# One transformer layer on one core: parameters packed by the host, the order of the first loads, and the stage's stored activations loaded by ScalarE's queue

## The chip, the core and the metric

The kernel runs on one core of a Trainium2 chip. The metric is the device time of one execution in microseconds (us). A core has five engines that work through their own instruction lists in order: TensorE (PE, matmuls), VectorE (DVE), ScalarE (ACT), GpSimd (POOL) and SyncE (SP, which here only issues DMAs). An engine whose instruction waits holds back everything behind it in its list. A DMA is issued by an instruction in some engine's list and then carried out by the core's 16 DMA engines.

## What is computed

One layer over 1024 tokens of width 1024: an adaptive RMSNorm, one projection that feeds eight attention heads and eight RWKV-7 heads, their output projection, and a PEER block, a feed-forward layer with 16,384 single-neuron experts of which each token uses 128.

```python
mod = silu(c) @ ada_w + ada_b                  # shift1, scale1, gate1, shift2, scale2, gate2
h   = rms_norm(x, norm1_g) * (1 + scale1) + shift1
z   = h @ w_in                                 # attention and RWKV-7 heads work on z
x   = x + gate1 * (concat(att, rw) @ w_out)
h2  = rms_norm(x, norm2_g) * (1 + scale2) + shift2
...
def block(args):                               # PEER, a block of 128 tokens; ic are the chosen experts
    u = take(expert_u, ic)
    act = gelu(einsum('cd,ced->ce', xc, u), approximate=False)
    vv = take(expert_v, ic)
    return einsum('ce,ced->cd', gc * act, vv)
```

## The kernel before

**The front** (0 to some 65 us). Small parameters are loaded one by one, each laid over partitions by the DMA itself: `scol` (L117) by SP, `bcol`, `g1col`, `mup`, `mun` and four pieces of `gqk` (L119 to L129) by ACT's queue, `w0`, `a0`, `kkc`, `kac`, `rkc` through `colp` (L319 to L322) by POOL's. DVE builds masks (`tables`), then multiplies sixteen 128x1024 pieces of `ada_w` (`adw`, L221) by silu(c) and adds them up in two tiles `macc`; 32 short matmuls (`mcol`) turn these into columns. SP loads the 16 pieces, two pieces of `w_in` (`wraw`) and then the eight row blocks of `x` (`xx`, L233). ACT squares each block of `x`, in list order behind the split of `wraw` (`wh`). After the statistics the blocks are scaled and transposed, and ACT and DVE write them as `hTh`, `hTl`, on which the projection works.

**The middle** (to some 2310 us) holds attention, the RWKV scans and the beginning of PEER.

**PEER** is computed in two ways at once. Token blocks 0 to 2 gather rows of the experts: POOL issues indirect DMAs `gu`, `gv` (128x1024 each, L1361), DVE multiplies and sums them (`gu` L1389, `gacc` L1397). Token blocks 3 to 7 (640 tokens) use dense products over all 128 tiles of 128 experts: `pact` = activations before the gelu (L314 to L316), `gl` = their gelu (ACT, L1460), times a gate `gt_` (POOL, L1771), split into `ah` (ACT, L1772) and `al` (DVE, L1773), and times the experts' value rows `vr`, split into `vh` (ACT, L1791) and `vl` (DVE, L1792), in the products `py` (L1812 to L1814), whose sums go into `yac` (DVE, L1821).

For 65 "early" tiles the gelu is computed in the middle and stored in DRAM (`actd`); `gate_load` (L1758) loads one back into a `gl` tile. `g_load` (L1763) loads the gates of four tiles, a `gt_` of 128x2560. The experts' inputs for the other tiles come as `u` (L1438), split into `uTh` (ACT) and `uTl` (DVE).

**The last stage** (2310 to 3820 us) walks through 32 groups of four tiles, mostly two early and two late ones. For one group TensorE runs: first half of the columns, four tiles of `py` (15 matmuls each); one late tile's `pact`; second half, four tiles of `py`; the other late tile's `pact`. There are five `py` banks, so a half can only begin when `yac` of the half before it is read out. The loop spreads each group's gathers over its eight steps, and an added dependency (`pace`, in `fetch` and `gate`) keeps a gather on POOL behind the gating multiplication before it.

The code is written in this loop's order, but the builder that closes the kernel orders each engine's instructions itself when the program is finished. So a load that changes engine can change the order on other engines too; the section on the change shows where.

Of the kernel before, what the change touches and what calls it, by code (L numbers as in the profile page):

```python
# [20 lines left out]
D = 1024  # L21
NB = 8
# [56 lines left out]
def body(tc, nc, I, out, dbg=None):  # L79
# [3 lines left out]
    with root:  # L83
# [3 lines left out]
        def ct(shape, name, dt=F32):  # L87
            return cst.tile(shape, dt, name=name)
# [31 lines left out]
        g1col = ct([128, NK], "g1col")  # L120
        nc.scalar.dma_start(g1col, I["norm1_g"][0].rearrange("(j p) -> p j", p=128))
        mup = ct([128, 14], "mup")
        nc.scalar.dma_start(mup, I["mu_prev"][0].rearrange("(j p) -> p j", p=128))
        mun = ct([128, 14], "mun")
        nc.scalar.dma_start(mun, I["mu_next"][0].rearrange("(j p) -> p j", p=128))
        gqk = ct([128, 2], "gqk")
        for i, nm in enumerate(("q_norm_g", "k_norm_g")):
            for h in range(2):
                nc.scalar.dma_start(gqk[64 * h:64 * h + 64, i:i + 1], I[nm][0].rearrange("(p o) -> p o", o=1))  # L129
        nc.scalar.activation(scol, scol, AF.Silu)  # L130
        nc.vector.tensor_scalar(gqk[:, 0:1], gqk[:, 0:1], HD ** -0.5, None, op0=ALU.mult)
# [15 lines left out]
        def slot(name, shape=(128, 1024), dt=F32):  # L147
            return sp[1].tile(list(shape), dt, name=name, tag="s")
# [77 lines left out]
        GO = [12, 8, 6, 9, 7, 10, 11, 0, 1, 2, 3, 4, 5]
        WT = {GO[0]: load_w(w_in, GO[0] * 256, nc.gpsimd)}
        xt = []
        ssq = small("ssq", [128, NB])
        rstd = small("rstd", [128, NB])  # L230
        for tb in range(NB):
            xx = slot("xx")
            nc.sync.dma_start(xx, x[tb * 128:(tb + 1) * 128, :])  # L233
            xt.append(xx)
            jk = slot("jk")
            nc.scalar.activation(jk, xx, AF.Square, accum_out=ssq[:, tb:tb + 1])
            if tb % 4 == 3:
                r_ = rstd[:, tb - 3:tb + 1]
                nc.vector.tensor_scalar(r_, ssq[:, tb - 3:tb + 1], 1.0 / D, 1e-6, op0=ALU.mult, op1=ALU.add)
                rsqrt(r_, r_, [128, 4], "r1")  # L240
                for b in range(tb - 3, tb + 1):
                    if b < 4:
                        nc.vector.tensor_scalar(xt[b], xt[b], rstd[:, b:b + 1], None, op0=ALU.mult)
                    else:
                        nc.scalar.activation(xt[b], xt[b], AF.Copy, scale=rstd[:, b:b + 1])
        mcol = bank("mcol", "po")
# [77 lines left out]
        w0 = [colp(f"w0{d}", I["w_decay0"][0][d], 4) for d in range(2)]
        a0 = [colp(f"a0{d}", I["a_gate0"][0][d], 4) for d in range(2)]
        kkc = colp("kkc", I["k_k"][0], 4)
        kac = colp("kac", I["k_a"][0], 4)
        rkc = colp("rkc", I["r_k"][0].rearrange("h e -> (h e)"), 4)
        ka1 = fc([128, 4], "ka1")
# [1571 lines left out]
```

## Time and profile before

| what | value |
| --- | --- |
| median of 3 runs | 3872.6 us (3858.38, 3872.6, 3874.69) |
| profiled execution, its own time | 3867.33 us |
| its span (first to last instruction) | 3865.2 us |
| TensorE clock granted, mean | 0.932 |
| busy: TensorE, VectorE, GpSimd, ScalarE | 85%, 78%, 45%, 34% |
| DMA share of SP's and ACT's transfers, of the gathers | 35.6%, 29.0% |

The span leaves 2.1 us outside. A granted clock of 1.00 is the higher of TensorE's two levels. Shares are means over stages with different limits: the front waits for transfers, the last stage is a loop in which TensorE, VectorE, GpSimd and the queues wait for one another in turn. The rows further down are read with this in mind: what a stage waits for last is what sets it.

### The profile page before, as it was taken

Reading aid. Unit: us, or ns where it says so; the run is one execution under the profiler, and the core shown is the slowest. Engines: PE = TensorE matmul, PEld = TensorE weight load, DVE = VectorE, ACT = ScalarE, POOL = GpSimd, SP = SyncE. Lnnn points to the kernel's source line nnn. Section 1 sums busy time; section 2 is a strip of 40 time slices with the busy share of each in tenths; the row PEclk is TensorE's granted clock in tenths of the full one; section 3 lists DMA queues with packets and bytes.
Section 4 is the critical chain, followed back from the end, with each engine's and each line's share of the span. In section 5 each row is a group of like instructions: output and inputs, shape, how many; then the busy total and the mean of one; then the engine's idle time right before and its main releaser. Section 6 shows DMA issues by size and latency. Waiting matters only on the chain. (4 is left out here: it accounts for less than half of the span.)

```text
span 3865.2 us, 59635 instructions
## 1 busy us (share of the span) xinstructions
PE 3298.5 (85%) x21937; PEld 2906.7 (75%) x21937; DVE 3004.1 (78%) x5970; ACT 1317.4 (34%) x2710; POOL 1754.6 (45%) x1346
## 2 busy tenths in 40 slices
PE   4968899899697988878878878888889889899998
PEld 4747887677586987877777877777777777777787
DVE  6785556767747799999998977777777878778776
ACT  3234334455212322222377873222222222222221
POOL 2032211222334455466754527555555565655541
PEclk9988999999798988999998999999999999999999
DMA  6434444433464357566798988777777877777774
GB/s 200 177 124 138 140 102 111 113 95 82 124 203 176 115 164 238 173 211 214 270 329 275 342 286 330 285 284 285 289 289 290 301 289 290 291 289 290 295 271 160
DMA packets 493451, 862.66 MB, mean 223 GB/s; under 512 B 149348, under 2 KB 290404, under 8 KB 489064
## 3 DMA queue, kind: packets, MB, share of 16 engines
q1 hardware_dynamic: 372840, 447.20, 35.6%
q0 software_dynamic: 113280, 411.63, 29.0%
q8 instruction: 173, 2.83, 0.3%
q10 hardware_dynamic: 7040, 0.03, 0.1%
q14 instruction: 118, 0.97, 0.1%
HBM read 741.91 MB, written 116.80 MB: 222 GB/s over the span
## 5 line engine op out<-in xcount | busy, mean ns | idle before, releaser
L316 PE MATMUL pact<-dTh,uTl 128*128 128x320 f32 x2048 | 646.2, 317 | 53.9 <-DVE uTl L1449 53.7
L314 PE MATMUL pact<-dTh,uTh 128*128 128x320 f32 x2048 | 648.4, 317 | 24.6 <-ACT uTh L1448 14.3
L315 PE MATMUL pact<-dTl,uTh 128*128 128x320 f32 x2048 | 644.1, 315 | 0.0
L1361 POOL DMA_INDIRECT gu<-in_peer_u_dram,ei x384 | 532.2, 1386 | 221.9 <-DVE gu L1389 135.2
L1389 DVE SCALAR_TENSOR_TENSOR gu<-gu,ghr 128x1024 f32<-128x1024 f32 x384 | 510.1, 1329 | 154.9 <-DMA gu<-in_peer_u_dram,ei 148.3
L1812 PE MATMUL py<-vh,ah 128*128 128x512 f32 x1280 | 522.1, 408 | 98.8 <-DVE yac L1821 58.2
L1813 PE MATMUL py<-vl,ah 128*128 128x512 f32 x1280 | 525.2, 410 | 65.4 <-DVE vl L1792 65.0
L1361 POOL DMA_INDIRECT gv<-in_peer_v_dram,ei x384 | 499.2, 1300 | 158.5 <-issue 89.0
L1397 DVE SCALAR_TENSOR_TENSOR gacc<-gv,gact,gacc 128x1024 f32<-128x1024 f32 x381 | 526.5, 1382 | 54.1 <-DMA gv<-in_peer_v_dram,ei 51.1
L1814 PE MATMUL py<-vh,al 128*128 128x512 f32 x1280 | 517.8, 405 | 2.8 <-DVE al L1773 2.8
L316 PEld LDWEIGHTS pact<-dTh,uTl 128*128 128x128 f32 x2048 | 393.7, 193 | 61.2 <-DVE uTl L1449 61.2
L314 PEld LDWEIGHTS pact<-dTh,uTh 128*128 128x128 f32 x2048 | 395.0, 193 | 30.7 <-ACT uTh L1448 15.8
L315 PEld LDWEIGHTS pact<-dTl,uTh 128*128 128x128 f32 x2048 | 394.1, 192 | 2.5
L1812 PEld LDWEIGHTS py<-vh,ah 128*128 128x128 f32 x1280 | 252.3, 197 | 160.3 <-ACT gl L1460 37.5
L1813 PEld LDWEIGHTS py<-vl,ah 128*128 128x128 f32 x1280 | 252.4, 197 | 139.7 <-DVE vl L1792 88.9
L1814 PEld LDWEIGHTS py<-vh,al 128*128 128x128 f32 x1280 | 252.5, 197 | 56.7 <-DVE al L1773 3.3
L1791 ACT ACTIVATE vh<-vr 128x512 fp32r<-128x512 f32 x256 | 155.9, 625 | 395.8 <-PE py L1814 377.3
L1772 ACT ACTIVATE ah<-gl 128x640 fp32r<-128x640 f32 x128 | 91.2, 735 | 461.2 <-POOL gl L1771 323.5
L1705 DVE TENSOR_TENSOR o<-io,tT 128x1024 f32<-128x1024 f32 x160 | 187.0, 1217 | 34.2 <-ACT tT L161 24.8
L1718 PE MATMUL pgb<-o,o 128*128 128x128 f32 x1280 | 178.4, 295 | 39.0 <-ACT o L1708 29.6
L1448 ACT ACTIVATE uTh<-u 128x1024 fp32r<-128x1024 f32 x128 | 135.1, 1056 | 215.6 <-PE pact L315 174.3
L1773 DVE TENSOR_TENSOR al<-gl,ah 128x640 fp32r<-128x640 f32 x128 | 104.0, 832 | 132.7 <-ACT ah L1772 132.5
(1438 smaller groups left out, 7130.2 us busy)
## 6 DMA issues: line engine op xcount, KB each, us to landing
u<-in_peer_ut_dram SPq DMA_DIRECT2D x128, 512.0 KB
vr<-in_peer_v_dram SPq DMA_DIRECT2D x256, 256.0 KB
Gd<-st SPq DMA_DIRECT2D x160, 256.0 KB
actd<-gl SPq DMA_DIRECT2D x65, 320.0 KB
gl<-actd SPq DMA_DIRECT2D x65, 320.0 KB
awt<-in_ada_w_dram SPq DMA_DIRECT2D x32, 512.0 KB
wraw<-in_peer_w_query_dram SPq DMA_DIRECT2D x32, 512.0 KB
wraw<-in_w_in_dram SPq DMA_DIRECT2D x26, 512.0 KB
```

The costliest lines, as they stand in the source:

```text
L314: nc.tensor.matmul(ps, lh, rh, start=(i == 0), stop=False)
L315: nc.tensor.matmul(ps, lh, rl, start=False, stop=False)
L316: nc.tensor.matmul(ps, ll, rh, start=False, stop=(i == n - 1))
L1361: g_ = nc.gpsimd.indirect_dma_start(out=r_, out_offset=None, in_=src, in_offset=bass.IndirectOffsetOnAxis(ap=eid[tb][:, j:j + 1], axis=0))
L1389: nc.vector.scalar_tensor_tensor(u, u, 1.0, hr, op0=ALU.mult, op1=ALU.mult, accum_out=act[:, q:q + 1])
L1397: nc.vector.scalar_tensor_tensor(acc, v, pact[:, q:q + 1], acc, op0=ALU.mult, op1=ALU.add)
L1705: nc.vector.tensor_tensor(o_, io128[:, None, :].to_broadcast([128, 8, 128]), tT[:, i, t0:t0 + 8, None].to_broadcast([128, 8, 128]), ALU.is ...
L1718: nc.tensor.matmul(pg[:, q * 128:(q + 1) * 128], o1[:, 4 * x_ + q], o2[:, 4 * x_ + q], start=True, stop=True)
L1791: nc.scalar.activation(vh, vts[i], AF.Copy)
L1812: nc.tensor.matmul(ys[hf][b], ah[:, ts], vh, start=(n == tiles[0]), stop=False)
L1813: nc.tensor.matmul(ys[hf][b], ah[:, ts], vl, start=False, stop=False)
L1814: nc.tensor.matmul(ys[hf][b], al[:, ts], vh, start=False, stop=(n == tiles[-1]))
```

## The change

Three things are changed. The host packs twelve kinds of small parameters into one array of 128x90, loaded by one DMA (`pk`) at the head of SP's list; the tiles of before are now slices of it, and `scol` and `gqk` are written from slices. In the front, the first four blocks of `x` are loaded and squared ahead of `ada_w`, and `ada_w` is taken by halves of columns (all eight row blocks of one half, then of the other). In the last stage `gate_load` and `g_load` issue from ACT's list and no longer from SP's.

```diff
+        pk = ct([128, 90], "pk")
+        nc.sync.dma_start(pk, I["pk"])
+        ccol, bcol, g1col, mup, mun, gqk_ = (cols(n) for n in (NK, 16, NK, 14, 14, 2))
+        w0, a0 = [cols(4) for _ in range(2)], [cols(4) for _ in range(2)]
+        kkc, kac, rkc = (cols(4) for _ in range(3))
         scol = ct([128, NK], "scol")
-        nc.sync.dma_start(scol, I["c"][0].rearrange("(o p) -> p o", p=128))
-        bcol = ct([128, 16], "bcol")
-        nc.scalar.dma_start(bcol, ada_b[0:2048].rearrange("(j p) -> p j", p=128))
...
-        nc.scalar.activation(scol, scol, AF.Silu)
+        nc.scalar.activation(scol, ccol, AF.Silu)
+        nc.vector.tensor_copy(gqk, gqk_)
...
+        def x_in(tbs):
+            for tb in tbs:
+                xx = slot("xx")
+                nc.sync.dma_start(xx, x[tb * 128:(tb + 1) * 128, :])
...
+        x_in(range(4))
 
         macc = [slot("macc") for _ in range(2)]
-        for k in range(NK):
-            for i in range(2):
+        for i in range(2):
+            for k in range(NK):
                 a = slot("adw")
...
         WT = {GO[0]: load_w(w_in, GO[0] * 256, nc.gpsimd)}
...
+        x_in(range(4, NB))
...
-        def colp(name, ap, n):
-            t_ = fc([128, n], name)
-            nc.gpsimd.dma_start(t_, ap.rearrange("(j p) -> p j", p=128))
-            return t_
...
         def gate_load(n):
             if n in early:
                 ats[n] = lpa.tile([128, TD], F32, name="gl", bufs=NGL)
-                nc.sync.dma_start(ats[n], actd[early.index(n)])
+                nc.scalar.dma_start(ats[n], actd[early.index(n)])
 
         def g_load(q):
             gts[q] = lp.tile([128, TD // TC, TA, TC], F32, name="gt_")
-            nc.sync.dma_start(gts[q], Gd[q])
+            nc.scalar.dma_start(gts[q], Gd[q])
```

In the rows below, a name's number only tells buffers apart; the same instruction has another number in the two kernels, and lines above L130 shift by a few.

**Where the loads of a group are issued.** SP's list before, from one load of `u` to the next, in a group of the last stage; `gl_30701` is the group's first stored tile, `gl_30730` its second:

```order
L1438 DMA u_30862<-in_peer_ut_dram 128x1024
L1785 DMA vr_30634<-in_peer_v_dram 128x512
L1785 DMA vr_30674<-in_peer_v_dram 128x512
L1785 DMA vr_30703<-in_peer_v_dram 128x512
L1761 DMA gl_30701<-actd_11964 128x640
L1785 DMA vr_30732<-in_peer_v_dram 128x512
L1765 DMA gt__31055<-Gd_18615 128x2560
L1761 DMA gl_30730<-actd_11964 128x640
L1785 DMA vr_30830<-in_peer_v_dram 128x512
L1438 DMA u_31044<-in_peer_ut_dram 128x1024
```

All the loads are in one list; each `vr` load waits for a `vl` that frees its buffer. After, SP's list of the same stretch:

```order
L1433 DMA u_30838<-in_peer_ut_dram 128x1024
L1780 DMA vr_30610<-in_peer_v_dram 128x512
L1780 DMA vr_30650<-in_peer_v_dram 128x512
L1780 DMA vr_30679<-in_peer_v_dram 128x512
L1780 DMA vr_30708<-in_peer_v_dram 128x512
L1433 DMA u_31020<-in_peer_ut_dram 128x1024
L1780 DMA vr_30806<-in_peer_v_dram 128x512
L1780 DMA vr_30844<-in_peer_v_dram 128x512
```

The two `gl` and the `gt_` are gone from it. They stand in ACT's list, where before there was, from a late tile's first gelu (`gl_30576<-pact_30577`) to the value splits:

```order
L1460 ACTIVATE gl_30576<-pact_30577 128x320
L1403 ACTIVATE gact_30085<-gact_30085 128x16
L1448 ACTIVATE uTh_30864<-u_30661 128x1024
L1460 ACTIVATE gl_30576<-pact_30603 128x320
L1772 ACTIVATE ah_30667<-gl_30576 128x640
L1772 ACTIVATE ah_30767<-gl_30701 128x640
L1791 ACTIVATE vh_30734<-vr_30634 128x512
L1791 ACTIVATE vh_30832<-vr_30674 128x512
L1791 ACTIVATE vh_30870<-vr_30703 128x512
```

and now is:

```order
L1455 ACTIVATE gl_30552<-pact_30553 128x320
L1756 DMA gl_30677<-actd_11940 128x640
L1398 ACTIVATE gact_30061<-gact_30061 128x16
L1443 ACTIVATE uTh_30840<-u_30637 128x1024
L1455 ACTIVATE gl_30552<-pact_30579 128x320
L1767 ACTIVATE ah_30643<-gl_30552 128x640
L1767 ACTIVATE ah_30743<-gl_30677 128x640
L1760 DMA gt__31031<-Gd_18591 128x2560
L1756 DMA gl_30706<-actd_11940 128x640
L1786 ACTIVATE vh_30710<-vr_30610 128x512
L1786 ACTIVATE vh_30808<-vr_30650 128x512
```

The first stored tile's load (`gl_30677`) stands right behind the first gelu, the gates and the second stored tile (`gl_30706`) behind the two `ah`.

**VectorE in the same group.** Before, from the two `al` to the first of the five `yac`; `vl_30735` is the operand of TensorE's fourth tile of the first half, whose sums are `py_30629` and on:

```order
L1773 TENSOR_TENSOR al_30668<-gl_30576,ah_30667 128x640
L1773 TENSOR_TENSOR al_30768<-gl_30701,ah_30767 128x640
L1792 TENSOR_TENSOR vl_30735<-vr_30634,vh_30734 128x512
L1389 SCALAR_TENSOR_TENSOR gu_30695,gact_30764<-gu_30695,ghr_27870 128x1024
L1397 SCALAR_TENSOR_TENSOR gacc_28618<-gv_30697,gact_30085,gacc_28618 128x1024
L1792 TENSOR_TENSOR vl_30833<-vr_30674,vh_30832 128x512
L1389 SCALAR_TENSOR_TENSOR gu_30724,gact_30764<-gu_30724,ghr_27870 128x1024
L1397 SCALAR_TENSOR_TENSOR gacc_28618<-gv_30726,gact_30085,gacc_28618 128x1024
L1821 TENSOR_TENSOR yac0_22364<-yac0_22364,py_30629 128x512
L1821 TENSOR_TENSOR yac1_22365<-yac1_22365,py_30630 128x512
```

After; the same operand is `vl_30711`, the same sums are `py_30605` and on:

```order
L1768 TENSOR_TENSOR al_30644<-gl_30552,ah_30643 128x640
L1768 TENSOR_TENSOR al_30744<-gl_30677,ah_30743 128x640
L1384 SCALAR_TENSOR_TENSOR gu_30671,gact_30740<-gu_30671,ghr_27846 128x1024
L1392 SCALAR_TENSOR_TENSOR gacc_28594<-gv_30673,gact_30061,gacc_28594 128x1024
L1384 SCALAR_TENSOR_TENSOR gu_30700,gact_30740<-gu_30700,ghr_27846 128x1024
L1787 TENSOR_TENSOR vl_30711<-vr_30610,vh_30710 128x512
L1787 TENSOR_TENSOR vl_30809<-vr_30650,vh_30808 128x512
L1392 SCALAR_TENSOR_TENSOR gacc_28594<-gv_30702,gact_30061,gacc_28594 128x1024
L1816 TENSOR_TENSOR yac0_22340<-yac0_22340,py_30605 128x512
L1816 TENSOR_TENSOR yac1_22341<-yac1_22341,py_30606 128x512
```

The `vl` of the fourth tile stood right behind the two `al`; now two `gu` and a `gacc`, each of which reads a gathered row, stand between them. Of the 30 places in the last stage where two `al` follow one another, 28 have this pattern. TensorE's own list and POOL's are the same in both kernels, from group to group, but for names.

## Rows read from the trace of the kernel before

**Rows 1.** The page, part 1: busy us (share of the span) xinstructions of each engine.

```profile
PE 3298.5 (85%) x21937; PEld 2906.7 (75%) x21937; DVE 3004.1 (78%) x5970; ACT 1317.4 (34%) x2710; POOL 1754.6 (45%) x1346
```

**Rows 2.** Windows of the front: stretch, us, busy us (count) per engine, PEclk, DMA share, GB/s.

```profile
4.00:6.00 2.00, 0.00 (x0) 0.00 (x0) 0.00 (x0) 0.00 (x0) 2.00 (x3) 1.00 1.04 83
...
10.00:12.00 2.00, 0.00 (x0) 0.00 (x0) 0.00 (x0) 0.00 (x0) 0.00 (x0) 1.00 0.98 181
...
24.00:32.00 8.00, 0.00 (x0) 0.00 (x0) 8.00 (x7) 0.00 (x0) 0.00 (x0) 1.00 1.02 418
```

**Rows 3.** Timeline of the front, VectorE, SyncE's queue, ScalarE: start us, us, engine, instruction, [idle before].

```profile
13.32 0.17 DVE L332 TENSOR_TENSOR mu<-mup,mun 128x14 f32<-128x14 f32 x1 [12.22 <-DMA mun<-in_mu_next_dram]
...
21.26 16.82 DVE L225 SCALAR_TENSOR_TENSOR macc<-adw,scol,macc 128x1024 f32<-128x1024 f32 x14
...
29.65 9.83 SPq L233 DMA_DIRECT2D xx<-in_x_dram  x8
...
51.41 0.78 ACT L261 ACTIVATE hTh<-pt,sb,sg 128x512 fp32r<-128x512 f32 x1 [0.19 <-PE pt L257]
```

**Rows 4.** Waits, 2400 to 3760 us: engine line waited for: us in total, times, longest.

```profile
POOL gl L1771 <- DMA gl<-actd: 223.8, 17, 18.1
DVE gu L1389 <- DMA gu<-in_peer_u_dram,ei: 133.1, 46, 5.4
...
PE py L1813 <- DVE vl L1792: 63.7, 44, 5.2
...
PE py L1812 <- DVE yac L1821: 52.1, 19, 4.4
```

**Rows 5.** Timeline of one group of the last stage: ScalarE, SyncE's queue, GpSimd.

```profile
3596.53 0.44 ACT L1460 ACTIVATE gl<-pact 128x320 f32<-128x320 f32 x1 [2.88 <-PE pact L316]
...
3589.46 9.81 SPq L1785 DMA_DIRECT2D vr<-in_peer_v_dram  x4
3599.32 0.42 SPq L1761 DMA_DIRECT2D gl<-actd  x1
3606.66 0.33 SPq L1765 DMA_DIRECT2D gt__32982<-Gd  x1
...
3610.00 0.44 SPq L1438 DMA_DIRECT2D u<-in_peer_ut_dram  x1
...
3603.54 1.57 POOL L1771 TENSOR_TENSOR gl<-gl,gt__32593 128x640 f32<-128x640 f32 x1 [15.76 <-issue]
...
3606.78 0.99 POOL L1361 DMA_INDIRECT gu<-in_peer_u_dram,ei  x1
```

**Rows 6.** The same group on VectorE.

```profile
3607.44 1.56 DVE L1773 TENSOR_TENSOR al<-gl,ah 128x640 fp32r<-128x640 f32 x2 [5.05 <-ACT ah L1772]
3608.92 0.68 DVE L1792 TENSOR_TENSOR vl<-vr,vh 128x512 fp32r<-128x512 f32 x1
3613.78 1.23 DVE L1389 SCALAR_TENSOR_TENSOR gu<-gu,ghr 128x1024 f32<-128x1024 f32 x1 [4.18 <-DMA gu<-in_peer_u_dram,ei]
...
3615.91 1.29 DVE L1397 SCALAR_TENSOR_TENSOR gacc<-gv,gact,gacc 128x1024 f32<-128x1024 f32 x1 [0.90 <-DMA gv<-in_peer_v_dram,ei]
...
3618.00 2.72 DVE L1389 SCALAR_TENSOR_TENSOR gu<-gu,ghr 128x1024 f32<-128x1024 f32 x1 [0.20 <-issue]
...
3621.85 3.07 DVE L1821 TENSOR_TENSOR yac<-yac,py 128x512 f32<-128x512 f32 x5
```

**Rows 7.** The same group on TensorE, matmul by matmul.

```profile
3610.07 0.39 PE L1812 MATMUL py<-vh,ah 128*128 128x512 f32 x1
...
3613.02 0.39 PE L1813 MATMUL py<-vl,ah 128*128 128x512 f32 x1
...
3622.67 0.47 PE L1812 MATMUL py<-vh,ah 128*128 128x512 f32 x1 [2.00 <-DVE yac L1821]
...
3627.78 0.39 PE L1812 MATMUL py<-vh,ah 128*128 128x512 f32 x1
```

**Rows 8.** Windows of the same group: one stretch right behind the eight gathers' first issues.

```profile
3609.00:3611.00 2.00, 2.00 (x11) 1.65 (x10) 0.60 (x2) 0.71 (x2) 1.39 (x3) 1.00 1.03 430
```

More of the change, by code (lines that the diff above doesn't have):

```diff
@@ L113, in body, with cols @@
         w_in = I["w_in"][0]
-        scol = ct([128, NK], "scol")
-        nc.sync.dma_start(scol, I["c"][0].rearrange("(o p) -> p o", p=128))
-        bcol = ct([128, 16], "bcol")
-        nc.scalar.dma_start(bcol, ada_b[0:2048].rearrange("(j p) -> p j", p=128))
[L120 to L125, printed above, removed]
+        pk = ct([128, 90], "pk")
+        nc.sync.dma_start(pk, I["pk"])
+        po_ = [0]
+        def cols(n):
+            po_[0] += n
+            return pk[:, po_[0] - n:po_[0]]
+        ccol, bcol, g1col, mup, mun, gqk_ = (cols(n) for n in (NK, 16, NK, 14, 14, 2))
+        w0, a0 = [cols(4) for _ in range(2)], [cols(4) for _ in range(2)]
+        kkc, kac, rkc = (cols(4) for _ in range(3))
+        scol = ct([128, NK], "scol")
         gqk = ct([128, 2], "gqk")
-        for i, nm in enumerate(("q_norm_g", "k_norm_g")):
-            for h in range(2):
-                nc.scalar.dma_start(gqk[64 * h:64 * h + 64, i:i + 1], I[nm][0].rearrange("(p o) -> p o", o=1))
-        nc.scalar.activation(scol, scol, AF.Silu)
+        nc.scalar.activation(scol, ccol, AF.Silu)
+        nc.vector.tensor_copy(gqk, gqk_)
         nc.vector.tensor_scalar(gqk[:, 0:1], gqk[:, 0:1], HD ** -0.5, None, op0=ALU.mult)
@@ L215, in body @@
         tables()
+        xt = []
+        ssq = small("ssq", [128, NB])
+        rstd = small("rstd", [128, NB])
+        def x_in(tbs):
+            for tb in tbs:
+                xx = slot("xx")
+                nc.sync.dma_start(xx, x[tb * 128:(tb + 1) * 128, :])
+                xt.append(xx)
+                jk = slot("jk")
+                nc.scalar.activation(jk, xx, AF.Square, accum_out=ssq[:, tb:tb + 1])
+                if tb % 4 == 3:
+                    r_ = rstd[:, tb - 3:tb + 1]
+                    nc.vector.tensor_scalar(r_, ssq[:, tb - 3:tb + 1], 1.0 / D, 1e-6, op0=ALU.mult, op1=ALU.add)
+                    rsqrt(r_, r_, [128, 4], "r1")
+                    for b in range(tb - 3, tb + 1):
+                        if b < 4:
+                            nc.vector.tensor_scalar(xt[b], xt[b], rstd[:, b:b + 1], None, op0=ALU.mult)
+                        else:
+                            nc.scalar.activation(xt[b], xt[b], AF.Copy, scale=rstd[:, b:b + 1])
+        x_in(range(4))
         macc = [slot("macc") for _ in range(2)]
-        for k in range(NK):
-            for i in range(2):
+        for i in range(2):
+            for k in range(NK):
                 a = slot("adw")
@@ L227, in body @@
         WT = {GO[0]: load_w(w_in, GO[0] * 256, nc.gpsimd)}
[L228 to L245, printed above, removed]
+        x_in(range(4, NB))
         mcol = bank("mcol", "po")
@@ L316, in mm3 @@
                 nc.tensor.matmul(ps, ll, rh, start=False, stop=(i == n - 1))
-        def colp(name, ap, n):
-            t_ = fc([128, n], name)
-            nc.gpsimd.dma_start(t_, ap.rearrange("(j p) -> p j", p=128))
-            return t_
[L324 to L328, printed above, removed]
         ka1 = fc([128, 4], "ka1")
@@ L1872, in body @@
         pe.close()
-_INS = ['x', 'c', 'ada_w', 'ada_b', 'norm1_g', 'w_in', 'mu_prev', 'mu_next', 'q_norm_g', 'k_norm_g', 'w_decay0',
-        'w_decay_up', 'a_gate0', 'a_gate_up', 'g_up', 'k_k', 'k_a', 'r_k', 'lnx_g', 'lnx_b', 'w_out', 'norm2_g',
+_INS = ['x', 'ada_w', 'ada_b', 'w_in',
+        'w_decay_up', 'a_gate_up', 'g_up', 'lnx_g', 'lnx_b', 'w_out', 'norm2_g',
         'peer_w_query', 'peer_sub_keys1', 'peer_sub_keys2', 'peer_u', 'peer_v']
@@ L1890 @@
         args[name] = nc.dram_tensor(f"in_{name}_dram", a.shape, mybir.dt.from_np(a.dtype), kind="ExternalInput").ap()
+    P = lambda n: _np.asarray(inputs[n])[0].reshape(-1)
+    a = [P("c"), P("ada_b")[:2048], P("norm1_g"), P("mu_prev"), P("mu_next")] + [P(n) for n in ("q_norm_g", "k_norm_g") for _ in range(2)]
+    a = _np.concatenate(a + [P(n) for n in ("w_decay0", "a_gate0", "k_k", "k_a", "r_k")])
+    a = _np.ascontiguousarray(a.reshape(-1, 128).T)
+    arrays["in_pk_dram"] = a
+    args["pk"] = nc.dram_tensor("in_pk_dram", a.shape, mybir.dt.from_np(a.dtype), kind="ExternalInput").ap()
     a = inputs["peer_u"]
```

## The prediction, written before the result was known

> **What bounds the kernel now.** I read the page's engine shares first, then the front by windows and timeline, then the waits of the last stage and one of its groups, engine by engine. TensorE is busy 85% of the span and VectorE 78% [rows 1]: neither is full, so the stages have to be read one by one.
>
> In the front the bound is the transfers. From 4 to 6 us the DMA engines are full (share 1.04) while they move 83 GB/s; from 10 to 12 us share 0.98, 181 GB/s; from 24 to 32 us share 1.02 and 418 GB/s [rows 2]. The engines are as busy with tiny pieces as later with large ones. VectorE sits idle for 12.22 us until `mun` lands [rows 3].
>
> The last stage, 2310 to 3820 us and the largest part of the span, is a loop. A late tile's first gelu (call its start G, here 3596.53) is followed on SyncE by the load of the group's first stored tile `gl` only at 3599.32, since SyncE first issues four `vr` loads from 3589.46 on, each behind a wait [rows 5]. 4.2 us later GpSimd multiplies it (3603.54), then the late tile, then issues the gathers (3606.78) [rows 5]. VectorE's two `al` start at 3607.44 (call this s = G + 10.9) and the `vl` behind them ends at 3609.6 [rows 6], in time for TensorE, whose fourth tile starts at 3610.07 = s + 2.6 without a wait [rows 7]. VectorE then has nothing until the first gathered row lands (gap of 4.18 us, `gu` at 3613.78 = s + 6.3), and its `yac` comes at 3621.85 [rows 6]. That makes TensorE wait 2.00 us, and the tile behind that wait takes 5.11 us (3622.67 to 3627.78) where one at full pitch takes 3.4 (13 steps from 3610.07 to 3613.02, 0.227 us each, times 15) [rows 7]. Over 2400 to 3760 us, 28 groups, TensorE waits 63.7 us for `vl` and 52.1 us for `yac` [rows 4]: 4.1 us a group, and some 2 us more through the slow matmuls behind the waits, 6.1 in all. VectorE waits 133.1 us for `gu` and GpSimd 223.8 us for `gl` [rows 4].
>
> **The change part by part. Front.** The tiny pieces go; `pk` is 128 rows of 360 bytes. What is left up to the last block of `x` is 16 pieces of `adw`, two of `wraw` and eight of `x`, 0.52 MB each: 13.6 MB, 34 us at an estimated 0.4 MB/us (418 GB/s was the best of these stretches [rows 2]). Before, this stream got going at about 14 us; now it can start at some 5 to 8 us. So the last block of `x` should land 6 to 9 us earlier. `hTh` (51.41 before) follows the squares of `x`, not VectorE: `macc` took 16.82 us for 14 pieces [rows 3] and now starts earlier and waits for arrivals, done some 10 us before the last `x` block is squared. Eight blocks were issued from 29.65 on [rows 3]; four go to the head now, which keeps ScalarE's squares off the end. I take -8 us, bounds -10 and -4. The list of the middle is unchanged but for names, so it should arrive at the last stage whole; bounds -10 and 0.
>
> **Loads on ScalarE.** 65 `gl` and 32 `gt_` move from SyncE to ScalarE. The first stored tile's load stands right behind the first gelu, 0.44 us long [rows 5], so it is issued at about G + 0.5: 2.3 us earlier in this group, and by my reading of other groups (0.6 to 3.5 us after G before) 1.8 us on average. The chain through GpSimd's multiplication moves with it: s = G + 8.8 instead of G + 10.6. The 97 issues cost ScalarE some 0.4 us each, as on SyncE [rows 5]; with three a group and ScalarE 34% busy [rows 1] that hides. The second stored tile's load waits on ScalarE for VectorE's `al`; queued behind are four `vh`. The `al` come right then (s to s + 1.56 [rows 6]), so at most 1 us, on `vh` whose `vl` is late now anyway: nothing, bounds 0 and +1 a group. At the stage's start two `gt_` leave their places among SyncE's loads: +-3 us once.
>
> **VectorE's list.** This is the term that decides. The `vl` of TensorE's fourth tile stood right behind the `al`. Now it stands behind `gu`, `gacc`, `gu`. The rows for these come from gathers that GpSimd issues from s - 0.7 on (3606.78 [rows 5]). If the gathers land as they do now, `gu` starts at s + 6.3, `gacc` at s + 8.5, the second `gu` at s + 10.6 and ends at s + 13.3 [rows 6], and the `vl` (0.68) at s + 13.9; a second group that I read gives some s + 12.4, so 13.1 on average. TensorE could start its fourth tile at s + 3.1 before (mean of s + 2.3 to s + 4.2), which is s + 4.9 by the earlier s. So it now waits 13.1 - 4.9 = 8.2 us, and this tile takes 1.7 us (as in rows 7) to 3 us longer, 2.2 taken. What disappears: while TensorE stands, VectorE gets ahead, `yac` then follows the fourth tile at once, under the 7 us of `pact`, and the 6.1 us of the second half go. Sum: 8.2 + 2.2 - 6.1 = +4.3 us a group; in 28 groups +120.
>
> Against that stands relief. Just behind the gathers' issue the DMA engines are full (share 1.03, 430 GB/s [rows 8]): a `gt_` (1.31 MB), a `gl` (0.33), a `vr` (0.26) and a `u` (0.52) go out within 4 us (3606.66 to 3610.00 [rows 5]), beside the gathers. In the new lists the `u` stands ahead of that point, and the `vr` waits for the `vl` that is late: 0.79 MB less, 1.9 us at 0.41 MB/us. If all of it reaches VectorE, `vl` ends at s + 11.2, the sum is +2.4 a group, +67; if also the second `gu` takes 1.23 us and not 2.72 [rows 6], +0.9, +25. The price of a gather on an empty path no row shows; if all rows were there at s + 5, `vl` ends at some s + 9, and the sum is -1.3 a group, -36. I take relief of 1.9 us, +67, since both of its causes are in the lists, and keep -36 and +120 as ends; with this group's own s + 13.9 and the slow tile at +3 it would be +160.
>
> Sum: 3867.3 (the profiled execution, 5.3 below the median of the three) - 8 + 67 = 3926.
>
> **The rivals.** *The load wins.* The gathers are there in time, the `vl` costs nothing, and s comes 1.8 us earlier in 28 groups: -50 - 8, 3809. For it: GpSimd's 223.8 us of waiting for `gl` [rows 4]. Against it: VectorE waits 4.18 us for the same gathers already, ahead of two more steps [rows 6], and TensorE's fourth tile did not wait for s at all in this group [rows 7]. It decides from `vl` ending before about s + 5.
>
> *Only the front.* What the late `vl` costs and what TensorE's second half gets back are equal: `vl` at some s + 9.7. Then 3867 - 8 = 3859; by the load's place nothing is won, since it was not last. SyncE's late issue [rows 5] shows what the place costs, 2.3 us, and nothing of how TensorE gains by it. The Trainium skill has a rule that speaks for this rival ("DMA: Bandwidth & Descriptors", section "Issuing engines are not separate DMA queues"): DMAs of any engine run on the same 16 DMA engines, and another issuing engine only saves the time of issuing. By that rule the move would be worth nothing here and the result 3859; the trace agrees on the shared engines (share 1.03 with both kinds in flight [rows 8]), but shows a wait ahead of the issue that the rule doesn't count.
>
> *No relief.* The gathers land as before or later, since ScalarE's `gt_` still goes out with them: +120 to +160 - 8, 3979 to 4019.
>
> **How the numbers follow.** A measurement of this kernel can tell about 0.5%, 19 us, from no change. Forecast with relief (tail +20 to +100): 0.52, 3880 to 3960. No relief: 0.22. Only the front: 0.15. The load wins: 0.11. So faster by over 0.5% 0.12, within 0.17, slower 0.71. The range leaves out "the load wins" and the upper part of "no relief": 3852 to 3990.
>
> **What would show it.** In the front: a first `macc` before 15 us, 13.6 MB done by about 42 us, the first `hTh` near 43.5. In the last stage: stored tiles' loads some 0.5 us after the gelu; on TensorE a wait at `py` for `vl` of 4 to 9 us once a group, at the fourth tile of the first half, and none for `yac`; on VectorE a wait for `py` ahead of `yac`. Wrong would be a `vl` total near the 63.7 us of before [rows 4], or VectorE's first `gu` behind the `al` starting by s + 4.

## The result: slower by 4.1%, and the profile after

The changed kernel takes 4022.9 us (median of four, 4021.73 to 4035.63), against 3870.55 us before: a ratio (of the means) of 1.0406, with a 95% interval of 1.0375 to 1.0438. The forecast was slower, 3926 us; the time lies above its range (3852 to 3990) and next to the rival *no relief* (3979 to 4019).

The profiled execution has a span of 4020.4 us. Page, part 1, as [rows 1]:

```profile
PE 3302.2 (82%) x21937; PEld 2920.1 (73%) x21937; DVE 3106.4 (77%) x5971; ACT 1324.0 (33%) x2710; POOL 1760.4 (44%) x1339
```

TensorE is busy as long as before (3302 against 3299 us); the 155 us are waiting. Its waits and those around it in the last stage, as [rows 4], from 2400 to 3900 us:

```profile
PE py L1808 <- DVE vl L1787: 273.0, 28, 11.8
DVE gu L1384 <- DMA gu<-in_peer_u_dram,ei: 183.2, 54, 6.6
...
POOL gl L1766 <- DMA gl<-actd: 111.1, 15, 10.8
DVE gacc L1392 <- DMA gv<-in_peer_v_dram,ei: 109.1, 56, 4.7
...
DVE al L1768 <- ACT ah L1767: 8.9, 4, 2.2
```

TensorE waits for `vl` 28 times, once a group, 9.75 us each: 273 us in place of 63.7; its wait for `yac` (52.1 before) is no longer among its larger waits. VectorE no longer waits for `ah` ahead of `al` (8.9 us; 105.0 before, in a row not shown): it comes late itself.

One group of the last stage, as [rows 5 to 7], on ScalarE and its queue, SyncE's queue, GpSimd, VectorE and TensorE:

```profile
3616.39 0.44 ACT L1455 ACTIVATE gl<-pact 128x320 f32<-128x320 f32 x1 [2.88 <-PE pact L321]
3616.40 0.33 ACTq L1756 DMA_DIRECT2D gl<-actd  x1
...
3624.06 0.33 ACTq L1760 DMA_DIRECT2D gt__32186<-Gd  x1
...
3626.26 0.33 SPq L1433 DMA_DIRECT2D u<-in_peer_ut_dram  x1
...
3619.53 1.96 POOL L1766 TENSOR_TENSOR gl<-gl,gt__31800 128x640 f32<-128x640 f32 x1 [8.58 <-DVE vl L1787]
...
3624.16 1.79 POOL L1356 DMA_INDIRECT gu<-in_peer_u_dram,ei  x1
...
3626.16 1.55 DVE L1768 TENSOR_TENSOR al<-gl,ah 128x640 fp32r<-128x640 f32 x2
3632.34 1.23 DVE L1384 SCALAR_TENSOR_TENSOR gu<-gu,ghr 128x1024 f32<-128x1024 f32 x1 [4.63 <-DMA gu<-in_peer_u_dram,ei]
...
3634.57 1.29 DVE L1392 SCALAR_TENSOR_TENSOR gacc<-gv,gact,gacc 128x1024 f32<-128x1024 f32 x1 [1.00 <-DMA gv<-in_peer_v_dram,ei]
3635.78 1.22 DVE L1384 SCALAR_TENSOR_TENSOR gu<-gu,ghr 128x1024 f32<-128x1024 f32 x1
...
3636.92 2.61 DVE L1787 TENSOR_TENSOR vl<-vr,vh 128x512 fp32r<-128x512 f32 x2
...
3640.65 0.68 DVE L1816 TENSOR_TENSOR yac<-yac,py 128x512 f32<-128x512 f32 x1
...
3638.99 0.80 PE L1808 MATMUL py<-vl,ah 128*128 128x512 f32 x1 [8.66 <-DVE vl L1787]
```

The first stored tile's load goes out with the gelu (3616.40), as forecast. GpSimd multiplies at 3619.53, and the gathers start at 3624.16, 0.1 us behind the gates' load (3624.06); the group's `u` goes out 2.1 us behind the first of them (3626.26). VectorE's `al` start at s = 3626.16, which is G + 9.8. Then it waits 4.63 us, and `gu`, `gacc`, `gu` and two `vl` follow, the two taking 2.61 us. TensorE's fourth tile stands 8.66 us. What the clock does then stands in two windows (columns as in [rows 2]):

```profile
3628.00:3630.00 2.00, 2.00 (x11) 1.59 (x9) 0.00 (x0) 0.58 (x2) 1.61 (x2) 1.00 1.00 401
...
3634.00:3636.00 2.00, 0.00 (x0) 0.00 (x0) 1.43 (x2) 0.00 (x0) 1.70 (x2) 0.50 1.02 418
```

The granted clock falls from 1.00 to 0.50, the lower of the two levels, while TensorE stands, so the tile behind the wait begins slow.

In the front, as [rows 3]:

```profile
2.83 0.17 DVE L327 TENSOR_TENSOR mu<-pk 128x14 f32<-128x14 f32 x1
...
28.95 11.19 DVE L247 SCALAR_TENSOR_TENSOR macc<-adw,scol,macc 128x1024 f32<-128x1024 f32 x7
...
44.28 0.78 ACT L266 ACTIVATE hTh<-pt,sb,sg 128x512 fp32r<-128x512 f32 x1 [1.76 <-DVE rstd L229]
```

`mu`, which is made of packed parameters, is at 2.83 us (13.32 before), `hTh` starts at 44.28 (51.41), so 7.1 us are won there. In this trace they don't last. Set against one another by instruction, TensorE's list runs 7 to 12 us ahead of before until 1200 us and is 0.9 us behind at 1300 us (first `pact`: 1301.3 against 1300.4). The last stage begins 5.2 us early (first `py` 2312.57 against 2317.74) and lasts 1707.8 us to the end of the span, where it lasted 1547.5: +160.3 us. The 5.2 us say little: in the nine traces with this front, the last stage begins between 2312.6 and 2334.5 us.

Where the front's gain goes, in three rows of before and the same three of after: SyncE's two loads of `u` near 1190 us, ScalarE's `uTh`, TensorE's first transposes of `hr`:

```profile
1190.52 0.84 SPq L1438 DMA_DIRECT2D u<-in_peer_ut_dram  x2
...
1214.67 1.99 ACT L1448 ACTIVATE uTh<-u 128x1024 fp32r<-128x1024 f32 x2
...
1220.71 1.97 PE L1516 MATMUL pt<-ident,hr 128*128 128x128 f32 x8 [11.71 <-DMA hr<-h2d]
```

```profile
1181.60 41.17 SPq L1433 DMA_DIRECT2D u<-in_peer_ut_dram  x2
...
1222.46 1.06 ACT L1443 ACTIVATE uTh<-u 128x1024 fp32r<-128x1024 f32 x1 [17.05 <-issue]
...
1231.47 5.30 PE L1511 MATMUL pt<-ident,hr 128*128 128x128 f32 x24 [31.83 <-DMA hr<-h2d]
```

The second load of `u` now waits 40 us, which holds up the loads of `hr` behind it on SyncE, and `uTh` starts after 17 us of idleness that no row explains (the trace has it wait for a semaphore of GpSimd, which it does not before).

### The profile page after: what moved, and what is told of

Its sections match the earlier page's. It is cut to its first block, busy times and chain, and to the rows that moved or that the text cites. A ratio compares the mean times of both kernels' runs of the same rounds, so it can differ in the third digit from the quotient of the medians.

```text
span 4020.4 us, 59597 instructions
## 1 busy us (share of the span) xinstructions
PE 3302.2 (82%) x21937; PEld 2920.1 (73%) x21937; DVE 3106.4 (77%) x5971; ACT 1324.0 (33%) x2710; POOL 1760.4 (44%) x1339
## 3 DMA queue, kind: packets, MB, share of 16 engines
q8 instruction: 173, 2.83, 0.3%
## 4 chain that ended last, share of the span: by engine, by line
PE 41%; DVE 24%; DMA 13%; issue 12%; POOL 7%; ACT 2%; SPq 1%; POOLq 0%; DVEq 0%; ACTq 0%
DMA gv<-in_peer_v_dram,ei 7%; PE py L1808 4%; PE py L1809 4%; PE py L1807 4%; DVE gacc L1392 3%; DVE gu L1384 3%; PE psz L319 3%; PE psz L320 3%; PE psz L321 3%; PE pact L321 3%; PE pact L319 3%; PE pact L320 3%; POOL gv L1356 3%; POOL gu L1356 2%; DVE ef L1625 2%
## 5 line engine op out<-in xcount | busy, mean ns | idle before, releaser
L1392 DVE SCALAR_TENSOR_TENSOR gacc<-gv,gact,gacc 128x1024 f32<-128x1024 f32 x381 | 585.7, 1537 | 134.7 <-DMA gv<-in_peer_v_dram,ei 126.1
L1384 DVE SCALAR_TENSOR_TENSOR gu<-gu,ghr 128x1024 f32<-128x1024 f32 x384 | 519.5, 1354 | 200.8 <-DMA gu<-in_peer_u_dram,ei 195.0
L1356 POOL DMA_INDIRECT gu<-in_peer_u_dram,ei x384 | 521.5, 1358 | 194.8 <-DVE gu L1384 109.9
L1816 DVE TENSOR_TENSOR yac<-yac,py 128x512 f32<-128x512 f32 x310 | 200.3, 682 | 39.9 <-PE py L1809 38.7
L1787 DVE TENSOR_TENSOR vl<-vr,vh 128x512 fp32r<-128x512 f32 x256 | 203.3, 805 | 18.8 <-ACT vh L1786 18.8
L1455 ACT ACTIVATE gl<-pact 128x320 f32<-128x320 f32 x256 | 109.1, 429 | 300.6 <-PE pact L321 179.6
```

The costliest lines, as they stand in the source:

```text
L1356: g_ = nc.gpsimd.indirect_dma_start(out=r_, out_offset=None, in_=src, in_offset=bass.IndirectOffsetOnAxis(ap=eid[tb][:, j:j + 1], axis=0))
L1384: nc.vector.scalar_tensor_tensor(u, u, 1.0, hr, op0=ALU.mult, op1=ALU.mult, accum_out=act[:, q:q + 1])
L1392: nc.vector.scalar_tensor_tensor(acc, v, pact[:, q:q + 1], acc, op0=ALU.mult, op1=ALU.add)
L1787: nc.vector.tensor_tensor(vl, vts[i], vh, ALU.subtract)
L1816: nc.vector.tensor_tensor(y_, y_, ys[hf][b], ALU.add)
```

## The experiments

Theory A: the last stage loses its time through VectorE's list alone. Rival B: the loads cost because they stand in ScalarE's list. "s" is the start of the two `al` and "G" that of the late tile's first gelu, as in the prediction. Means over groups are mine, from the timelines between 2450 and 3750 us (23 to 28 groups a run).

### One part alone

`e1_front_only`: packed parameters and the order of the first loads.

```diff
-                nc.scalar.dma_start(ats[n], actd[early.index(n)])
+                nc.sync.dma_start(ats[n], actd[early.index(n)])
...
-            nc.scalar.dma_start(gts[q], Gd[q])
+            nc.sync.dma_start(gts[q], Gd[q])
```

> The packed parameters and the order of the first loads, with the stored tiles and gates loaded by SyncE as before; VectorE's list in the last stage is then that of before. Theory A (the loss is VectorE's list alone): first hTh near 44.3 as in the changed kernel, last stage as before, so 3870.5 - 7 = 3863 us, TensorE's wait for vl some 64 us. Rival B (the loads on ScalarE's queue cost by themselves): the same here. A third reading, C (the earlier front collides with something later): above 3880.

3866.57 us, ratio 0.9985 (0.9971 to 0.9998), TensorE's wait for `vl` 62.3 us. The front costs nothing in the last stage. Its gain is 5.9 us between the medians, 0.8 to 11 by the interval: too wide to tell the 8 us of the forecast from a part of them.

`e4_act_only`: the front of before, both kinds of loads by ScalarE.

> The front of before, with stored tiles and gates loaded by ScalarE: VectorE's list as in the changed kernel (gu, gacc, gu ahead of vl). Both theories: the two parts add up, so 4023 + 7 = 4030 us, 28 waits of TensorE for vl with some 270 us. If the front and the loads hang together, it is off by more than 10 us.

4027.02 us, ratio 1.0408 (1.0376 to 1.0439); 28 waits for `vl`, 271.5 us. The loss belongs to the move of the loads, and the parts add up.

### Which load: the same queue, other lists

`e2_gl_act` takes back only the gates' line of the diff above, `e3_gt_act` only the stored tiles'. In both, ScalarE issues loads; only in the second is VectorE's `vl` moved.

> The changed kernel with only the stored tiles (gl) loaded by ScalarE, the gates (gt_) by SyncE. VectorE's list is then as before: vl stands right behind the two al. Theory A: the loss is gone whole, and the first stored tile is loaded earlier: between 3813 and 3863 us, TensorE waits for vl under 80 us. Rival B: two of the three loads of a group still hold up ScalarE, so at least half of the 155 us stays: above 3930 us.

3838.7 us, ratio 0.9913 (0.9886 to 0.994): faster than both kernels, with 65 loads on ScalarE. Waits of GpSimd, VectorE and TensorE, as [rows 4], 2400 to 3760 us:

```profile
POOL gl L1766 <- DMA gl<-actd: 129.7, 12, 16.8
...
DVE gu L1384 <- DMA gu<-in_peer_u_dram,ei: 110.0, 38, 5.8
...
PE py L1808 <- DVE vl L1787: 86.8, 33, 5.2
...
PE py L1807 <- DVE yac L1816: 17.9, 14, 4.0
```

GpSimd waits 129.7 us for `gl` where it waited 223.8; TensorE's waits for `vl` and `yac` are 105 us together (116 before), those for `vl` alone a little over the 80 expected. VectorE's list in the stage is that of before, and s comes at G + 9.5, where it came at G + 11.1. So rival B falls for the stored tiles. For the gates it is not tested by itself: no run has them in ScalarE's list with `vl` in its old place.

> The changed kernel with only the gates (gt_) loaded by ScalarE, the stored tiles by SyncE. VectorE's list has the vl of the fourth tile behind one gu and one gacc (one gathered pair), not behind gu, gacc, gu. Theory A: vl ends some s + 10.4 instead of s + 13, TensorE waits some 7 us a group for it, 200 us in all: 3940 to 3970 us. Rival B: one of three loads moved, at most a third of the loss: under 3920 us.

4033.15 us, ratio 1.0422 (1.0394 to 1.045). One moved load, the full loss, with one gathered pair ahead of `vl` instead of three steps. That is more than theory A gave. A group on VectorE, with a multiplication of GpSimd and TensorE's fourth tile:

```profile
3415.12 1.56 DVE L1768 TENSOR_TENSOR al<-gl,ah 128x640 fp32r<-128x640 f32 x2 [4.88 <-ACT ah L1767]
3422.37 1.22 DVE L1384 SCALAR_TENSOR_TENSOR gu<-gu,ghr 128x1024 f32<-128x1024 f32 x1 [5.68 <-DMA gu<-in_peer_u_dram,ei]
...
3423.75 3.30 DVE L1392 SCALAR_TENSOR_TENSOR gacc<-gv,gact,gacc 128x1024 f32<-128x1024 f32 x1
3426.97 1.28 DVE L1787 TENSOR_TENSOR vl<-vr,vh 128x512 fp32r<-128x512 f32 x2
...
3424.42 1.54 POOL L1766 TENSOR_TENSOR gl<-gl,gt__30262 128x640 f32<-128x640 f32 x1
...
3427.71 0.79 PE L1808 MATMUL py<-vl,ah 128*128 128x512 f32 x1 [10.91 <-DVE vl L1787]
```

`gacc` takes 3.30 us instead of some 1.28: it runs beside GpSimd's multiplication (3424.42 to 3425.96), and `vl` ends at s + 12.5. Of 24 groups, `vl` ends by s + 10.5 in the twelve where `gacc` takes 1.28 us, and at s + 12.5 to 14.1 in the twelve where it takes 2.0 to 3.3; the mean is s + 11.6, not 10.4, and TensorE waits 269.3 us in all. That is still less than the s + 13.0 of the changed kernel; what makes the two equal stands behind the next runs.

### The order alone, with every load where it was

`e5_before_late` and `e6_before_late2` are the kernel before; an added dependency holds the fourth tile's `vl` behind one `gu`, or behind `gu`, `gacc`, `gu`. The lines are e5's; e6 also takes one more gathered pair in this step and one fewer in the next.

```diff
-                nc.vector.tensor_tensor(vl, vts[i], vh, ALU.subtract)
+                v_ = nc.vector.tensor_tensor(vl, vts[i], vh, ALU.subtract)
+                if i % 8 == 3 and ulast[0] is not None:
+                    tc.add_manual_dep(v_.ins, ulast[0].ins.name,
...
-                    vs[4 * x_ + y_]()
+                    late_ = g > 1 and now[0] % 8 == 3
+                    if not late_:
+                        vs[4 * x_ + y_]()
                     if now[0] >= GS0:
                         gathers(GR / 8.0 * left / (NT - GEND - GS0 * GR / 8.0))
+                    if late_:
+                        vs[4 * x_ + y_]()
```

> The kernel before, all loads and the front untouched; in each group of the last stage from the third on the value split vl of TensorE's fourth tile is put behind one gu on VectorE (one gathered row), and nothing else moves. Theory A (VectorE's list alone sets the loss): vl ends some s + 8.5, TensorE waits 4 to 6 us a group for it and no longer for yac: 3890 to 3930 us. Rival B (the loads on ScalarE's queue are what costs): 3865 to 3880 us, as before.

3975.98 us, ratio 1.0273 (1.0237 to 1.031).

```profile
PE py L1818 <- DVE vl L1793: 194.6, 27, 11.4
```

> The kernel before with vl of the fourth tile behind gu, gacc, gu, as in the changed kernel, and all loads on SyncE as before; one more gathered pair is handled in that step and one fewer in the next. Theory A: the whole loss without the change: 4010 to 4040 us, 28 waits of TensorE for vl with some 270 us. Rival B: 3865 to 3880 us; a mixture of both: in between.

4087.08 us, ratio 1.0561 (1.0544 to 1.0579).

```profile
PE py L1818 <- DVE vl L1793: 317.4, 28, 12.6
```

With no load moved, the place of one instruction a group costs as much as the change and more. Theory A's direction is shown, rival B is not needed, and the sizes were too small both times: in e5 (`vl` ends at s + 9.5 on average) 108 us and not 20 to 60, in e6 (s + 14.5) 219 and not 140 to 170.

The two edits do more than their text says, in two ways. In seven of the 28 groups, all in the first half of the stage, e5 has `gu`, `gacc`, `gu` ahead of `vl` and e6 five steps. And a late `vl` holds up SyncE's `vr` loads, and the stored tile's load stands behind them in the same list; a group of e5:

```profile
3485.03 0.44 ACT L1461 ACTIVATE gl<-pact 128x320 f32<-128x320 f32 x1 [2.88 <-PE pact L316]
...
3476.70 14.16 SPq L1786 DMA_DIRECT2D vr<-in_peer_v_dram  x4
3490.91 0.42 SPq L1762 DMA_DIRECT2D gl<-actd  x1
...
3495.23 1.56 POOL L1772 TENSOR_TENSOR gl<-gl,gt__31055 128x640 f32<-128x640 f32 x1 [13.61 <-DMA gl<-actd]
```

The load goes out 5.9 us after the gelu, and GpSimd waits for it. Groups 15 to 28 of the stage are free of the first point (one `gu` in each group of e5, `gu`, `gacc`, `gu` in each of e6) and show the second; means in us:

| groups 15 to 28 | before | e2 | e5 | after | e3 | e6 |
| --- | --- | --- | --- | --- | --- | --- |
| stored tile's load, after G | 1.5 | 0.0 | 4.0 | 0.0 | 3.9 | 3.7 |
| s, after G | 11.1 | 9.5 | 13.9 | 11.9 | 13.6 | 13.5 |
| end of `vl`, after s | 2.2 | 2.2 | 8.3 | 13.1 | 11.7 | 13.4 |
| end of `vl`, after G | 13.2 | 11.7 | 22.2 | 25.0 | 25.2 | 26.9 |
| length of a group on TensorE | 48.6 | 47.8 | 52.5 | 55.3 | 55.6 | 57.2 |

Where `vl` is late, a group is as long as `vl` ends after G, and 30.3 us more, to 0.1 us in all four runs. So the end of `vl` sets the stage's length, wherever the delay comes from: from the place in VectorE's list, or from a later s. The changed kernel loses less than e6 because its stored tile's load does not stand behind `vr`, and e3 loses as much as the changed kernel with fewer steps ahead of `vl` because its load does.

### Why the relief did not come

`e7_after_nogt` loads the gates once.

```diff
-            nc.scalar.dma_start(gts[q], Gd[q])
+            if q < 1:
+                nc.scalar.dma_start(gts[q], Gd[q])
+            else:
+                gts[q] = gts[0]
```

> The changed kernel with the gates gt_ loaded once, for the first group, and used for all groups (the output is another one): 1.3 MB a group less to load. VectorE's list is then as before, so it is to be held against the run with only the stored tiles on ScalarE (3838.7 us; gu read 7.0 us after the first gather's issue). Theory R (the gathers wait for the other loads; the relief of the prediction was a matter of size): gu is read under 5 us after the issue, 3790 to 3825 us. Rival (the gathers take that long by themselves): 6.3 to 7.3 us after it, 3825 to 3840 us.

3796.35 us, ratio 0.9812 (0.9796 to 0.9829); up to 3760 us:

```profile
PE py L1811 <- DVE vl L1790: 78.6, 36, 3.5
...
DVE gu L1384 <- DMA gu<-in_peer_u_dram,ei: 47.6, 24, 4.5
```

VectorE waits 47.6 us for `gu`, where e2 has 110.0; `gu` is read 5.2 us after the first gather's issue, against 8.0 in e2 and 7.4 before (under 5 was expected, the rival asked for 6.3 and more; groups whose rows had landed before are left out; the expectations' 7.0 and 4.7 pass over a first gather that goes out more than 3 us ahead of s). So the gathers do wait for other bytes. Those bytes are the gates', which are issued 0.1 us ahead of the gathers both before (3606.66 against 3606.78 [rows 5]) and after. Before, the `u` and the `vr` of the prediction went out 3 us behind the first gather [rows 5]. In the changed kernel `vr` is gone from there, but `u` still goes out behind the gather in 19 of 23 groups, and the rows come later, not sooner: `gu` is read 9.4 us after the first gather's issue. Why it is 2 us more than before stays open; in e4, with the same lists, it is 9.2.

`e9_gl_gtl0`, `e10_gl_gtl1`, `e11_gl_gtl2`: e2, with the gates' load held behind later `vr` loads in SyncE's list.

```diff
-            nc.sync.dma_start(gts[q], Gd[q])
+            l_ = nc.sync.dma_start(gts[q], Gd[q])
+            if vld[0] is not None:
+                tc.add_manual_dep(l_.ins, vld[0].ins.name,
...
```

In e10 and e11 `g_load` is also called one and two of the loop's steps later.

> The run with both stored tiles on ScalarE and the gates on SyncE (3838.7 us), and in SyncE's list the gates' load put behind the next u and the next vr, whose buffer the vl at s + 2 frees: issued at some s + 2.5 and not at s - 0.8. VectorE's list as before. If the gates' 1.3 MB ahead of the gathers set when gu lands (the run with gates loaded once: 4.7 us after the issue, 3796 us): gu read 5 to 6.5 us after the first gather's issue, 3815 to 3835 us. If not: 3835 to 3845 us.

> As the run before, with the gates' load one vr further back, behind the vl that follows the first gathered pair: issued some 8 to 10 us after s, behind the burst of gathers. If the gates stand in the gathers' way: gu read under 5.2 us after the issue, 3800 to 3825 us. If what is won there is lost at the next gathers: 3830 to 3845 us.

> As the run before, another vr further back: the gates come some 15 us after s. Same expectation, 3800 to 3825 us; if the load now meets the second half's gathers instead, 3825 to 3845 us.

3811.6 us, ratio 0.9872 (0.9836 to 0.9907); 3817.69 us, 0.9885 (0.9858 to 0.9912); 3871.69 us, 1.0021 (1.0003 to 1.004). The load came later than I wrote; in e9, by `al`, the gates' load and the multiplication that uses it:

```profile
3607.29 1.55 DVE L1772 TENSOR_TENSOR al<-gl,ah 128x640 fp32r<-128x640 f32 x2
...
3635.69 0.38 SPq L1760 DMA_DIRECT2D gt__33338<-Gd  x1
...
3647.63 2.00 POOL L1770 TENSOR_TENSOR gl<-gl,gt__33338 128x640 f32<-128x640 f32 x1 [12.17 <-DMA gl<-actd]
```

That is s + 28, 12 us ahead of its use. `gu` is read 5.2 us after the issue (e9), 4.6 (e10), 4.4 (e11): the gates were in the gathers' way. e9 is faster than expected, e10 as expected, and e11 is a miss: the load goes out so late that GpSimd waits for `gt_` 21 times, 337 us in all up to 3900 us, which uses up the gain.

### Where the front's gain goes

Theory D: the wait of SyncE's `u` for the stores of `h2d` eats it. In the build of `e12_pack_ki`, the front with `ada_w` taken in the old order (k outside, i inside), that load doesn't wait for them.

> The front alone (loads of the last stage on SyncE as before), and ada_w taken in the old order of its pieces: packed parameters and x's half in front stay. In the run of the whole front, SyncE's second load of u near 1190 us waits 40 us for the stores of h2d, so that transposes of hr start 12 us later than before; in this build that load does not wait for them. Theory D (this wait eats the front's gain): hr's first transposes some 7 us earlier than before (1214 us), and the ratio to before 0.9975 to 0.9985. Rival: the gain is lost elsewhere too, the ratio is that of the whole front (0.9985) or nearer to 1.

3864.29 us, ratio 0.9992 (0.9978 to 1.0006): the rival's.

```profile
1187.40 0.85 SPq L1433 DMA_DIRECT2D u<-in_peer_ut_dram  x2
...
1210.63 22.55 SPq L1503 DMA_DIRECT2D hr<-h2d  x3
...
1228.25 2.00 ACT L1443 ACTIVATE uTh<-u 128x1024 fp32r<-128x1024 f32 x2 [17.05 <-issue]
```

Both loads of `u` go out at once, and still the gain is gone at TensorE's first `pact` (1303.6 us, 1300.4 before): `uTh` starts 17.05 us late, the second wait of the pair above. In the instruction lists, `uTh` waits for GpSimd and one of its DMAs in e1, e12 and after, and for neither in before. Theory D named half of it. `e13_best` has e12's front with e9's loads:

> All that helped: packed parameters, x's half in front, ada_w in the old order, stored tiles loaded by ScalarE, the gates by SyncE behind the next u and vr. Theory D with what the other runs showed: some 10 us under the run without the old order of ada_w (3811.6 us, ratio 0.9872), so ratio 0.983 to 0.986, 3795 to 3808 us. Rival (the wait for h2d was covered): 0.987.

3811.21 us, ratio 0.9858 (0.9838 to 0.9878): no better than e9; the ratio is just inside the expected range, the time above it.

Theory E: both waits together. `e14_pack_only` keeps of the front only the packed parameters; its lists have neither wait.

```diff
-        x_in(range(4))
...
-        for i in range(2):
-            for k in range(NK):
+        for k in range(NK):
+            for i in range(2):
...
-        x_in(range(4, NB))
+        x_in(range(NB))
```

> Of the change only the packed parameters: x behind ada_w and ada_w in its order, as before, the loads of the last stage on SyncE. In this build neither SyncE's load of u nor ScalarE's uTh near 1200 us waits for the stores of h2d. Theory E (these two waits ate the front's gain): whatever the front wins (first psz matmul 5 to 7 us before 63.4) is still there at 1300 us and at the last stage's first py, and the ratio is 0.9975 to 0.9985. Rival: the gain is gone at 1300 us here too.

3855.73 us, ratio 0.9958 (0.994 to 0.9975).

```profile
1209.75 1.99 ACT L1442 ACTIVATE uTh<-u 128x1024 fp32r<-128x1024 f32 x2
...
1215.84 1.97 PE L1510 MATMUL pt<-ident,hr 128*128 128x128 f32 x8 [11.76 <-DMA hr<-h2d]
```

The first `psz` is at 55.06 (63.41 before; 56.36 in the changed kernel), so packing alone wins as much in the front as the whole change did. `hr` is 4.9 us early, the first `pact` 4.0, the last stage's first `py` 7.2 (2310.6). The time is 13.8 us under before, more than the front can give; of the 13.7 us between the two traces, 6.5 are a shorter last stage (1541.0 against 1547.5) with the same lists, so scatter. The interval lies clear of e12's and just touches e1's.

Single traces scatter by several us by 1190 us (SyncE's first `u` at 1189.8 to 1196.6 in the four with the front of before). A stretch within each trace shows the two waits apart from that, from this first `u` to TensorE's first `pact`: 109.8 to 110.3 us in those four, 119.0 to 119.7 in the nine with the whole new front, 116.1 and 116.8 in e12 and e13, 110.8 and 110.2 in e14 and e15. Both waits together cost 9.3 us there, the second alone some 6.5. `e15_best2` adds e9's loads:

> The packed parameters as in the run before, with stored tiles loaded by ScalarE and the gates by SyncE behind the next u and vr. Theory E: the gains add up, ratio 0.980 to 0.985. Rival: 0.986 to 0.987, as with the whole front.

3808.13 us, ratio 0.9818 (0.9795 to 0.9842), the fastest kernel here with the whole computation. Its interval overlaps e9's.

## Why the prediction was wrong

**Right.** The direction, the place and the mechanism: `vl` behind gathered rows, one TensorE wait a group at the fourth tile, none for `yac` of any weight, and the first load with the gelu. The order in VectorE's list (e5, e6) and the queue without it (e2) show it. The front's gain is there at 44 us (7.1 us).

**The step that failed: the relief.** The prediction's wait at the fourth tile was 8.2 us without relief and 6.3 with it; measured are 9.75. Put into its own scheme, 9.75 + 2.2 - 6.1 is 5.85 us a group, 164 us in 28 groups, and the last stage grew by 160. So the wait is the term that was wrong. `gu` is read 6.74 us after s on average (6.57 before), where relief asked for some 4.7. The `u` that was to stand ahead of the gathers goes out behind the first of them in most groups, so 0.52 of the 0.79 MB did not leave the stretch; and I counted which loads leave it and not which stand ahead of the first gather: e7 and e9 show that the 1.3 MB ahead are worth 2.8 us.

**A second term: s did not come earlier.** The list gave s = G + 8.8. Measured are 11.2 after and 11.1 before. The tile is there sooner: GpSimd's second multiplication ends 8.5 us after G, 10.1 before. But the `al` start 2.7 us behind it and not 1.0, and no longer wait for `ah`: VectorE, after standing with TensorE, is behind with its own list. The 1.8 us for the earlier load were counted as if its taker were free; without them and without relief the prediction's wait is 10.0 us. In e2, where VectorE is not behind, s comes 1.6 us earlier and the load wins 28 us beside e1. That is also where the rival *only the front* fell: what the load gained is its place in a list with no wait ahead of it. The rule of the Trainium skill named there ("DMA: Bandwidth & Descriptors", section "Issuing engines are not separate DMA queues"), on the time of issuing alone, leaves that out.

The rival *no relief* came within 4 us of the result, in part by luck: it had s 1.8 us too early, and its upper end, +160, took the longest `vl` and the slowest tile of one group in place of that.

**A third: what one late instruction costs.** e5 put `vl` 7.3 us later and cost 3.9 us a group, where the scheme of the prediction (9.5 - 3.1 + 2.2 - 6.1) gives 2.5. It kept s in its place; in e5 s comes at G + 13.2, 2.1 us later than before, by SyncE's list. It also took TensorE's second-half waits as won back; in e5 they come back in part as waits for `vh` (32 us). Two figures of the prediction do not follow from its own terms: with `vl` at s + 9, 9 - 4.9 + 2.2 - 6.1 is +0.2 a group and not -1.3, and cost and gain are equal at s + 8.8, not 9.7. Neither enters the 3926.

**The front** was sized right; "should arrive at the last stage whole" rested on an unchanged list. The list was unchanged but for names; the waits attached to two instructions were not, and I had not read those. That the new waits come from where the builder puts these tiles (`u` and `uTh` over tiles that the stores of `h2d` still read) is argued from the names of the waits, not shown by itself. Shown is the stretch of 119 us in place of 110 in every trace that has both waits; how much of the 8 us is left at the end, the times don't resolve (e1: 5.9, interval 0.8 to 11). `e8_e1_act`, only the first stored tile on ScalarE, was to tell what e2 wins by:

> The changed kernel with only the first stored tile of each group loaded by ScalarE, the second and the gates by SyncE; VectorE's list as before. If the gain of the run with both stored tiles on ScalarE (3838.7 us) is that the first one is loaded right behind the gelu: 3833 to 3846 us, POOL's wait for gl well under that of before. If it came from the second: 3856 to 3868 us, as with the front alone.

3843.81 us, ratio 0.994 (0.9924 to 0.9957): most of it is the first tile; the rest of e2's gain lies within the intervals.

## What to carry to other kernels

Where a builder orders the lists, moving a load to another queue is a change of every list: compare each engine's order, and the waits on each instruction, before and after. An instruction that another engine needs at once must not stand behind one that waits for a transfer; here one subtraction of 0.7 us, misplaced once a group, cost 2.7 to 5.6%, in part through the loads that it held up in another list. When you count on less traffic, see that the loads do leave the place, and look first at what stands ahead of the transfer that is waited for: here 1.3 MB ahead were worth 2.8 us.

## What the hardware showed that I had not expected

A VectorE operation of two SBUF inputs beside a GpSimd multiplication can be longer by about that multiplication: `gacc` 3.30 us in e3 against 1.28, beside a multiplication of 1.54 us; the `gu` of 2.72 us in [rows 6] (1.23 otherwise) stands beside one of 1.58 us (in a row not shown). In the last stage of before, the 19 `gacc` that lie beside a multiplication for over 0.6 us take 2.54 us in the median, the 242 beside none 1.28. In other places the multiplication is the longer one, up to 2.6 us against 1.57 alone. `yac`, which adds from PSUM, shows nothing of it: 0.67 us with and without. The Trainium skill ("SBUF — State Buffer", section "Terms") has the two engines share a pair of ports that one holds for a whole instruction while the other blocks; the extra 1.5 us of `gu` agrees with a block of about that length. The extra 2.0 us of e3's `gacc`, which had begun 0.67 us ahead of the multiplication, is more than that and stays open. It is part of why e3, with one gathered pair ahead of `vl`, lost as much as the change with three steps ahead.
